# Weight sums of a seven-product scheme moved from VectorE into accumulating DMA transfers

## The chip, the cores and the metric

The kernel runs on one core of a Trainium2 chip. The metric is the device time of one execution in microseconds. TensorE does the matmuls, VectorE (DVE), ScalarE (ACT) and GpSimd (POOL) the elementwise work. Transfers are issued by SyncE (its queue is SP) and in a few places by GpSimd (its queue is POOL); all of them are carried out by the same 16 DMA engines of the core.

## The reference, cut to what matters

One inference step of a decoder layer on 576 tokens (512 of a prompt, 64 of a sample group). An RMS-normalised input is multiplied by the wide matrix `w_in`; its columns are split into attention, indexer, convolution and gate parts, and the two branches are merged and projected:

```python
c = split_columns(rms_norm(x, ln_g) @ w_in)        # 2048 x 10312
...
branch_attn = (attn * silu(c['z_attn'])) @ w_up_attn           # 1024 x 2048
u = c['glu_val'] * sigmoid(c['glu_gate'])                      # then a depthwise convolution over u
...
branch_conv = (conv_out * silu(c['z_conv'])) @ w_up_conv
merged = sigmoid(c['gate_attn']) * branch_attn + sigmoid(c['gate_conv']) * branch_conv
y = x + merged @ w_out
```

All values are float32. The kernel computes each float32 product as three matmuls: each operand is split into a high part (a cast to fp32r) and the remainder, and high x high, high x low and low x high are added.

## The kernel before

**Split.** `split` (lines 159 to 167) takes a weight tile `raw` of 128 partitions x 8 x 128: ACT casts it to `whi` (line 164) and DVE subtracts to make `wlo` (line 166). Both have three buffers, shared by everything that multiplies weights.

**Ordinary blocks.** `block` (line 248 has its matmul) multiplies such units with the normalised input for 576 tokens as two matmuls (256 and 320 columns) per weight and part. It is used up to about 660 us and from 1122 us on between the other products.

**Seven-product pairs.** `strassen` computes two neighbouring column blocks of 128 (`ca`, `cb`) for all tokens at once. The contraction is cut in two halves (`half` 0 and 1, `n` = 8 units of 128 rows each, 4 for `w_up_attn`) and the tokens in two halves of 288. The four weight quarters are b11 (half 0, ca), b12 (half 0, cb), b21 (half 1, ca) and b22 (half 1, cb). Seven products, each with one sum of weight quarters and one sum of input quarters (made once beforehand, lines 941 to 958 and 1083 to 1099), take the place of eight; a product is 24 matmuls of 288 columns (12 for `w_up_attn`; line 191). Its results are combined on DVE (line 201) and two copies on ACT (lines 205 and 210). The order is A11, S1, S2, S4, A12, S3, A22.

Four 512 KB loads from SP (line 178) bring the quarters, two into the two buffers of `wraw`, two into the two of `wx`. Four DVE instructions make the weight sums: t1 = b12 - b11 (line 207), t2 = b22 - t1 (212), b22 - b12 (217) and b21 - t2 (224).

There are 20 pairs over `w_in` (one for `z_conv`, three in the last three convolution tiles, eight for `gate_attn`, eight for `gate_conv`), which run back to back from 660 to 1122 us, and 8 pairs over `w_up_attn`, which alternate with ordinary blocks between 1155 and 1320 us. Beside the 20 pairs DVE also computes the depthwise convolution (`dw`, line 716) and the layer norm after it.

**Other transfers from GpSimd.** The attention gathers cache rows with indirect transfers on POOL (line 408): 128 rows of 1 KB each (`kic`, 128 KB) or 128 rows of 4 KB (`vc` and `kc`, 512 KB). Between 660 and 1600 us GpSimd has nothing to do.

**Order of the work.** The program gives each instruction a priority (`pri`): 0 for loading, summing and splitting weights, 1 for evictions, 3 and 5 for the attention and the convolution, 6 for the matmuls. The framework simulates the engines when it builds the program and fixes each engine's order by these priorities; on the chip each engine and each queue works in that order.

Of the kernel before, what the change touches and what calls it, by code (L numbers as in the profile page):

```python
# [9 lines left out]
F32 = mybir.dt.float32  # L10
# [4 lines left out]
OP = mybir.AluOpType  # L15
# [70 lines left out]
def build(tc, I, O):  # L86
    nc = tc.nc
    v, s, g, pe = nc.vector, nc.scalar, nc.gpsimd, nc.tensor
    dma = nc.sync.dma_start
# [3 lines left out]
    @contextmanager  # L93
    def pri(level):
        old = tc.cur_priority
        start = level * 1000000 + count.get(level, 0)
        tc.cur_priority = start
        yield
        count[level] = count.get(level, 0) + tc.cur_priority - start
        tc.cur_priority = old  # L100

    def ap(h, off, dims):
        return bass.AP(tensor=h.tensor, offset=h.offset + off, ap=[list(d) for d in dims])

    per = ctx.enter_context(tc.tile_pool(name="per", bufs=1))
# [63 lines left out]
    def strassen(pool, w, width, ca, cb, A, ev, kts=16, lvl=6, EV=1, rp=None):  # L169


        n = kts // 2
        with pri(0):
            raws = []
            for c0, half, tag in ((ca, 0, "wraw"), (cb, 0, "wraw"), (ca, 1, "wx"), (cb, 1, "wx")):
                t = (per.tile([128, 8, 128], F32, name="wraw", tag="wraw", bufs=2) if tag == "wraw" else
                     (rp or pool).tile([128, 8, 128], F32, name="wx", tag="wx", bufs=2))[:, :n]
                dma(t, ap(w, half * n * 128 * width + c0, [[width, 128], [128 * width, n], [1, 128]]))
                raws.append(t)
            b11, b12, b21, b22 = raws  # L180
            t1 = pool.tile([128, n, 128], F32, name="t1", tag="wt", bufs=2)
            t2 = pool.tile([128, n, 128], F32, name="t2", tag="wt", bufs=2)

        def product(raw, x):
            p = ps.tile([128, 512], F32, name="mms", tag="mm", bufs=4)[:, :T2]
            with pri(0):
                hi, lo = split(raw)
            with pri(lvl):
                for k in range(n):
                    for j, (a, part) in enumerate(((hi, 0), (hi, 1), (lo, 0))):  # L190
                        pe.matmul(p, a[:, k], A[x](part, k), start=(k == 0 and j == 0), stop=(k == n - 1 and j == 2))  # L191
            return p

        def kept():
            return pool.tile([128, T2], F32, name="sk", tag="sk", bufs=5)

        k1, k5, u2, v2 = (kept() for _ in range(4))

        def add(out, a, b):
            with pri(EV):  # L200
                v.tensor_add(out, a, b)  # L201

        p = product(b11, "A11")
        with pri(EV):
            s.copy(k1, p)
        with pri(0):
            v.tensor_sub(t1, b12, b11)
        p = product(t1, "S1")
        with pri(EV):
            s.copy(k5, p)  # L210
        with pri(0):
            v.tensor_sub(t2, b22, t1)
        p = product(t2, "S2")
        add(u2, p, k1)
        p = product(b22, "S4")
        with pri(0):
            v.tensor_sub(b22, b22, b12)
        add(v2, u2, k5)
        add(v2, p, v2)
        with pri(EV):  # L220
            ev(0, 1, v2)
        p = product(b21, "A12")
        with pri(0):
            v.tensor_sub(b21, b21, t2)
        add(k1, p, k1)
        with pri(EV):
            ev(0, 0, k1)
        p = product(b22, "S3")
        add(u2, p, u2)
        add(k5, u2, k5)  # L230
        with pri(EV):
            ev(1, 1, k5)
        p = product(b21, "A22")
        add(u2, p, u2)
        with pri(EV):
            ev(1, 0, u2)
# [47 lines left out]
    with tc.tile_pool(name="p0", bufs=1) as p0, pri(-1):  # L284
# [11 lines left out]
        def load(i):  # L296
            for cs in (slice(0, D // 2), slice(D // 2, D)):
                dma(xt[i][:TILES[i][1], cs], xrows(i)[:, cs])
# [27 lines left out]
        for h, tiles in enumerate(((0, 1), (2, 3, 4))):  # L326
            for i in tiles:
                n = TILES[i][1]
                for k, (eng, c0, c1) in enumerate(SQ[i]):
                    x, out = xt[i][:n, c0:c1], ss[:n, i, k:k + 1]  # L330
# [7 lines left out]
            with pri(-2):  # L338
# [7 lines left out]
                for c0, c1, eng in SCALE:  # L346
                    for k, i in enumerate(tiles):
                        x = xt[i][:TILES[i][1], c0 * 128:c1 * 128]
                        n = TILES[i][1]
                        (g if eng == "P" else v).tensor_scalar(x, x, rr[:n, k:k + 1], rt[:n, k:k + 1],  # L350
                                                               op0=OP.mult, op1=OP.mult)
            for kt in range(16):
                tag = PT_TAGS[h][kt % len(PT_TAGS[h])]
                pt = ps.tile([128, 512], F32, name="pt", tag=tag, bufs={"mm": 4, "w": 3, "o": 1}[tag])
                for i in tiles:
                    t0, n = TILES[i]
# [9 lines left out]
        for q in range(4):  # L366
            rows = slice(q * 32, (q + 1) * 32)
# [12 lines left out]
    CH, TK, EV = 3, 5, 1  # L380
# [31 lines left out]
    p = block(I["w_in"], D_IN, C_KI, xin, 72, units=units)  # L412
# [12 lines left out]
    with pri(CH):  # L425
# [15 lines left out]
        wt = p1.tile([128, 4, 8], F32, name="wt", tag="qh", bufs=2)  # L441
# [17 lines left out]
    for c in range(4):  # L459
        p = ps.tile([128, 512], F32, name="mm1", tag="mm", bufs=4)  # L460
# [8 lines left out]
        with pri(EV):  # L469
            s.copy(qi[:, c], p[:, NW:NQ])  # L470
            for e in range(2):
                rows = slice(e * 64, (e + 1) * 64)
# [107 lines left out]
    for kv in range(2):  # L580
        p = win(C_K + 128 * kv)
# [353 lines left out]
    with pri(CH):  # L935
        for q in range(4):
            c = slice(2 * q, 2 * q + 2)
            fs = [p4.tile([128, 2, T2], F32, name="f", tag="f", bufs=4) for _ in range(4)]
            whole(fs[0], quarter(1, 0), c)
            whole(fs[1], quarter(1, 1), c)  # L940
            v.tensor_add(fs[1], fs[0], fs[1])
            whole(fs[2], quarter(0, 0), c)
            parts(s1, fs[1], c)
            v.tensor_sub(fs[2], fs[1], fs[2])
            whole(fs[3], quarter(0, 1), c)
            parts(s2, fs[2], c)
            v.tensor_sub(fs[3], fs[3], fs[2])
            parts(s4, fs[3], c)
        for q in range(4):
            c = slice(2 * q, 2 * q + 2)  # L950
            f0, f1 = (st("f").rearrange("p (k t) -> p k t", k=2) for _ in range(2))
            whole(f0, quarter(0, 0), c)
            whole(f1, quarter(1, 0), c)
            v.tensor_sub(f0, f0, f1)
            parts(quarter(1, 0), f0, c)
# [116 lines left out]
    with pri(CH):  # L1072
        for k in range(4):
            t1, t2 = st("al"), st("al")
            dma(t1, a_d[k])
            dma(t2, a_d[k + 4])
            x11, x21, x12, x22 = t1[:, TS2[0]], t1[:, TS2[1]], t2[:, TS2[0]], t2[:, TS2[1]]

            def put(name, src):
                o = UA[name]  # L1080
                s.copy(o[:, 0, k], src)
                v.tensor_sub(o[:, 1, k], src, o.bitcast(F32)[:, 0, k])

            def new():
                return pU.tile([128, T2], F32, name="sk", tag="sk", bufs=5)

            f1, f2, f3, f4 = (new() for _ in range(4))
            put("A11", x11)
            v.tensor_sub(f3, x11, x21)
            put("S3", f3)  # L1090
            v.tensor_add(f1, x21, x22)
            put("S1", f1)
            v.tensor_sub(f2, f1, x11)
            put("S2", f2)
            put("A12", x12)
            put("A22", x22)
            v.tensor_sub(f4, x12, f2)
            put("S4", f4)
    XU = {a: (lambda part, k, o=o: o[:, part, k]) for a, o in UA.items()}
    cT = per.tile([128, 2, 8, T], R, name="cT", tag="x1")  # L1100
# [190 lines left out]
```

## Time and profile before

| | |
|---|---|
| runs (3) | 1604.26 to 1605.88 us, median 1605.86 us |
| profiled execution, its time | 1602.39 us |
| its span, first to last instruction | 1600.5 us |
| mean granted TensorE clock | 0.992 of full |
| data moved by DMA | 228.96 MB |

The profile lists for each engine how long it was busy and what it waited for. "PE" is TensorE's matmul side, "PEld" its weight loads, which overlap the matmuls. A busy TensorE says little by itself, since matmuls are pipelined; how many matmuls a stretch holds says more.

### The profile page before, as it was taken

How to read it: one execution, taken by the hardware profiler on the slowest of the kernel's cores; microseconds unless marked ns; L12 is line 12 of the kernel's file. 1: busy time of each engine (PE TensorE's matmuls, PEld its weight loads, DVE VectorE, ACT ScalarE, POOL GpSimd, SP SyncE). 2: the span in 40 equal slices, each digit the busy share in tenths (PEclk: the TensorE clock that was granted, in tenths of full speed). 3: DMA queues.
4: the chain of work that ended last, by engine and by line, in shares of the span. 5: the costliest groups of instructions: out<-in, count | busy, mean ns of one | idle time of the engine just before them, and what ended most of it. 6: DMA issues, size and time to landing. Idle time of an engine off the chain costs nothing.

```text
span 1600.5 us, 28485 instructions
## 1 busy us (share of the span) xinstructions
PE 1562.8 (98%) x11474; PEld 1517.9 (95%) x11474; DVE 1186.8 (74%) x2051; ACT 694.8 (43%) x1169; POOL 60.8 (4%) x81
## 2 busy tenths in 40 slices
PE   7999999999999999999999999999999999999997
PEld 5889999899989999999999999999999999999996
DVE  5436996365849599999999999899877675445554
ACT  5444324535455432344343345657533232334443
POOL 4200100101111000000000000000000000000000
PEclk8999999999999999999999999999999999999998
DMA  6632534434444334334343453644655666855773
GB/s 197 184 110 67 173 112 123 135 103 129 135 140 118 87 85 113 111 111 124 91 123 94 137 164 110 182 121 133 198 176 173 195 199 189 257 162 145 209 199 107
DMA packets 323827, 228.96 MB, mean 143 GB/s; under 512 B 15317, under 2 KB 293973, under 8 KB 322976
## 3 DMA queue, kind: packets, MB, share of 16 engines
q1 hardware_dynamic: 321008, 217.71, 46.6%
q0 software_dynamic: 2688, 9.44, 1.8%
q8 instruction: 90, 1.47, 0.4%
q14 instruction: 41, 0.34, 0.1%
HBM read 193.53 MB, written 36.96 MB: 144 GB/s over the span
## 4 chain that ended last, share of the span: by engine, by line
PE 88%; DVE 6%; issue 2%; DMA 2%; ACT 1%; POOL 0%; ACTq 0%; DVEq 0%; POOLq 0%
PE mm L248 51%; PE mms L191 26%; PE mm L467 2%; DVE wlo L166 2%; PE po L796 1%; DVE dw L716 1%; PE po L865 1%; PE pw L778 1%; DMA wx<-in_w_pw 1%; DVE sk L201 1%; PE pw L792 1%; PE pw L1209 1%; PE pw L527 1%; PE pw L828 0%; PE pt L357 0%
## 5 line engine op out<-in xcount | busy, mean ns | idle before, releaser
L248 PE MATMUL mm<-x,whi 128*128 128x256 f32 (+2 forms) x2368 | 430.6, 298 | 0.0
L248 PEld LDWEIGHTS mm<-x,whi 128*128 128x128 f32 (+1 forms) x2368 | 358.6, 187 | 5.8 <-issue 3.9
L164 ACT CAST whi<-wraw 128x1024 fp32r<-128x1024 f32 (+2 forms) x154 | 157.3, 1022 | 282.5 <-PE mm L248 203.5
L248 PE MATMUL mm<-x,wlo 128*128 128x256 f32 (+3 forms) x1184 | 260.3, 297 | 0.0
L191 PE MATMUL mms<-x,whi 128*128 128x288 f32 x1280 | 255.4, 296 | 4.3 <-DVE x L933 1.7
L166 DVE TENSOR_TENSOR wlo<-wraw,whi 128x1024 fp32r<-128x1024 f32 (+2 forms) x154 | 183.4, 1191 | 86.6 <-ACT whi L164 86.0
L164 ACT CAST whi<-wx 128x1024 fp32r<-128x1024 f32 (+1 forms) x156 | 150.0, 962 | 196.9 <-PE mm L248 53.4
L166 DVE TENSOR_TENSOR wlo<-wx,whi 128x1024 fp32r<-128x1024 f32 (+1 forms) x156 | 173.3, 1111 | 64.9 <-ACT whi L164 62.6
L191 PEld LDWEIGHTS mms<-x,whi 128*128 128x128 f32 x1280 | 204.5, 189 | 6.0 <-DVE x L933 2.1
L248 PE MATMUL mm<-m,whi 128*128 128x320 f32 (+1 forms) x1024 | 208.0, 298 | 0.0
L248 PEld LDWEIGHTS mm<-x,wlo 128*128 128x128 f32 (+1 forms) x1184 | 198.5, 187 | 0.7 <-issue 0.2
L191 PE MATMUL mms<-x,wlo 128*128 128x288 f32 x640 | 188.0, 297 | 3.5 <-DVE wlo L166 3.5
L191 PE MATMUL mms<-s,whi 128*128 128x288 f32 x960 | 191.4, 295 | 0.0
L716 DVE SCALAR_TENSOR_TENSOR dw<-u,cp,dw 128x512 f32<-128x512 f32 x240 | 178.2, 749 | 1.5
L248 PEld LDWEIGHTS mm<-m,whi 128*128 128x128 f32 x1024 | 164.3, 189 | 0.1
L191 PEld LDWEIGHTS mms<-s,whi 128*128 128x128 f32 x960 | 153.3, 188 | 0.1
L248 PE MATMUL mm<-m,wlo 128*128 128x320 f32 (+1 forms) x512 | 151.2, 296 | 0.0
L191 PE MATMUL mms<-s,wlo 128*128 128x288 f32 x480 | 140.9, 296 | 0.9 <-DVE wlo L166 0.9
L191 PEld LDWEIGHTS mms<-x,wlo 128*128 128x128 f32 x640 | 120.0, 189 | 5.3 <-DVE wlo L166 5.2
L164 ACT CAST whi<-t 128x1024 fp32r<-128x1024 f32 (+1 forms) x56 | 51.9, 927 | 110.5 <-PE mm L248 59.5
L248 PEld LDWEIGHTS mm<-m,wlo 128*128 128x128 f32 x512 | 96.4, 188 | 0.0
L191 PEld LDWEIGHTS mms<-s,wlo 128*128 128x128 f32 x480 | 89.9, 188 | 1.6 <-DVE wlo L166 1.5
(317 smaller groups left out, 2283.5 us busy)
## 6 DMA issues: line engine op xcount, KB each, us to landing
wraw<-in_w_in SPq DMA_DIRECT2D x120, 512.0 KB
wx<-in_w_in SPq DMA_DIRECT2D x40, 512.0 KB
wraw<-in_w_out SPq DMA_DIRECT2D x32, 512.0 KB
wx<-in_w_out SPq DMA_DIRECT2D x32, 512.0 KB
ga<-ga_d SPq DMA_DIRECT2D x32, 288.0 KB
ga_d<-gt SPq DMA_DIRECT2D x16, 288.0 KB
gc_d<-gt SPq DMA_DIRECT2D x16, 288.0 KB
gc<-gc_d SPq DMA_DIRECT2D x16, 288.0 KB
```

What stands on the lines that cost most here:

```text
L164: s.copy(hi, raw[:, :, :n])
L166: v.tensor_sub(lo, raw[:, :, :n], hi.bitcast(F32))
L191: pe.matmul(p, a[:, k], A[x](part, k), start=(k == 0 and j == 0), stop=(k == n - 1 and j == 2))
L201: v.tensor_add(out, a, b)
L248: pe.matmul(p[h][:n, :HN[h]], a[:, k, :n], x(part, kt, h), start=(kt == 0 and j == 0), stop=(kt == kts - 1 and j == 2))
L467: pe.matmul(p[:, :NQ], a[:, k], xk(part, kt)[:, 128:], start=(kt == 0 and j == 0), stop=(kt == 15 and j == 2))
L527: pe.matmul(d0[:, :W], qdup(part, h)[:, (i - 1) * 128:i * 128], kst[:, :W], start=(part == 0), stop=(part == 1))
L716: v.scalar_tensor_tensor(o1, a1, k1, o1, op0=OP.mult, op1=OP.add)
L778: pe.matmul(S[:, :max(W, 256)], a, x[:, kv, :max(W, 256)], start=(j == 0), stop=(j == 2))
L792: pe.transpose(pt[:, b * 128:(b + 1) * 128], Lt[:, b * 128:(b + 1) * 128], ident)
L796: pe.matmul(out[:, i * 128:(i + 1) * 128], vt[:, b, kv * 128:(kv + 1) * 128], PT[:, b * 128:(b + 1) * 128], start=(b == 0), stop=(b == i))
L865: pe.matmul(out[q:q + 32, :128], PT[:, r, q:q + 32], vc[:, b2, r * 256 + kv * 128:r * 256 + kv * 128 + 128], start=(r == 0), stop=False, t ...
```

## The change

The quarters b11, b21 and b22 are loaded from SP as before, and a tile `t` is loaded with b12. All weight sums are then made in place by DMA transfers that add what they read from HBM to what stands in the tile (`accum_op=OP.add`), issued by GpSimd: t += b11 gives the weight of S1; after S1's split t += b22 gives that of S2; after S2's split t += b21 gives that of A22; and after S4's split b22 += b12 gives that of S3. So that there are sums only, some signs change: two of the sums of input quarters and two of the combinations of products turn from an addition to a subtraction or the other way round. The order of the products becomes A11, S1, S4, S2, A12, S3, A22. The tag `wx` now has one tile per pair in its two buffers, `wt` too; `wraw` two as before.

```diff
+        def load(tile, half, c0):
+            dma(tile, rows(half, c0))
+            return tile
+
+        def more_of(tile, half, c0):
+            with pri(0):
+                g.dma_start(out=tile, in_=rows(half, c0), accum_op=OP.add)
...
+            b11 = load(shape(per, "wraw"), 0, ca)
+            t = load(shape(pool, "wt", n), 0, cb)
+            more_of(t, 0, ca)
+            b22 = load(shape(rp or pool, "wx"), 1, cb)
+            b21 = load(shape(per, "wraw"), 1, ca)
...
         p = product(b11, "A11")
         with pri(EV):
             s.copy(k1, p)
-        with pri(0):
-            v.tensor_sub(t1, b12, b11)
-        p = product(t1, "S1")
+        p = product(t, "S1")
+        more_of(t, 1, cb)
         with pri(EV):
             s.copy(k5, p)
-        with pri(0):
-            v.tensor_sub(t2, b22, t1)
-        p = product(t2, "S2")
+        p = product(b22, "S4")
+        more_of(b22, 0, cb)
+        add(v2, p, k5)
+        p = product(t, "S2")
+        more_of(t, 1, ca)
         add(u2, p, k1)
-        p = product(b22, "S4")
-        with pri(0):
-            v.tensor_sub(b22, b22, b12)
-        add(v2, u2, k5)
-        add(v2, p, v2)
+        sub(v2, v2, u2)
         with pri(EV):
             ev(0, 1, v2)
         p = product(b21, "A12")
-        with pri(0):
-            v.tensor_sub(b21, b21, t2)
         add(k1, p, k1)
...
         p = product(b22, "S3")
         add(u2, p, u2)
-        add(k5, u2, k5)
+        sub(k5, k5, u2)
...
-        p = product(b21, "A22")
+        p = product(t, "A22")
         add(u2, p, u2)
...
-            v.tensor_add(fs[1], fs[0], fs[1])
+            v.tensor_sub(fs[1], fs[0], fs[1])
...
-            v.tensor_sub(fs[3], fs[3], fs[2])
+            v.tensor_add(fs[3], fs[3], fs[2])
...
-            v.tensor_add(f1, x21, x22)
+            v.tensor_sub(f1, x21, x22)
...
-            v.tensor_sub(f4, x12, f2)
+            v.tensor_add(f4, x12, f2)
```

## Rows read from the trace of the kernel before

**Rows 1.** The page: busy time by engine; the chain by engine.
```profile
PE 1562.8 (98%) x11474; PEld 1517.9 (95%) x11474; DVE 1186.8 (74%) x2051; ACT 694.8 (43%) x1169; POOL 60.8 (4%) x81
...
PE 88%; DVE 6%; issue 2%; DMA 2%; ACT 1%; POOL 0%; ACTq 0%; DVEq 0%; POOLq 0%
```

**Rows 2.** Windows of the two stages with pairs (660:1122, 1155:1320).
```profile
core 0: us, PE busy (x) PEld busy (x) DVE busy (x) ACT busy (x) POOL busy (x), PEclk, DMA share, GB/s
660.00:1122.00 462.00, 453.29 (x3378) 448.89 (x3378) 439.63 (x611) 221.82 (x328) 0.00 (x0) 1.00 0.43 124
...
1155.00:1320.00 165.00, 160.39 (x1180) 158.38 (x1179) 122.81 (x232) 58.11 (x100) 0.00 (x0) 0.99 0.60 181
```

**Rows 3.** Windows of 40 us inside the first stage, same columns.
```profile
840.00:880.00 40.00, 37.44 (x280) 36.73 (x278) 38.78 (x53) 15.25 (x22) 0.00 (x0) 1.00 0.35 94
920.00:960.00 40.00, 40.00 (x304) 40.00 (x303) 37.36 (x51) 17.77 (x25) 0.00 (x0) 1.00 0.56 164
```

**Rows 4.** Waits of PE, 660:1122: us in total, times, longest us.
```profile
PE mms L191 <- DVE wlo L166: 4.4, 7, 1.2
PE mms L191 <- DVE x L933: 1.7, 2, 1.4
PE mms L191 <- ACT sk L210: 1.6, 2, 0.8
PE mms L191 <- ACT whi L164: 1.1, 2, 0.6
```

**Rows 5.** DVE's groups by line, 660:1122: count, busy us, mean ns, idle before.
```profile
L166 DVE TENSOR_TENSOR wlo<-wx,whi 128x1024 fp32r<-128x1024 f32 x80 | 97.5, 1219 | 4.4 <-ACT whi L164 4.3
L716 DVE SCALAR_TENSOR_TENSOR dw<-u,cp,dw 128x512 f32<-128x512 f32 x101 | 74.9, 746 | 0.0
...
L217 DVE TENSOR_TENSOR wx<-wx,wraw 128x1024 f32<-128x1024 f32 x20 | 24.4, 1219 | 0.1
```

**Rows 6.** ACT's waits, 660:1122, for its casts of weights.
```profile
ACT whi L164 <- PE mms L191: 74.2, 46, 2.5
...
ACT whi L164 <- DVE wx L217: 22.6, 8, 4.4
ACT whi L164 <- DVE t L212: 15.3, 11, 4.1
ACT whi L164 <- DVE wx L224: 9.6, 5, 3.1
```

**Rows 7.** ACT's groups by line, 660:1122.
```profile
L164 ACT CAST whi<-wx 128x1024 fp32r<-128x1024 f32 x80 | 83.9, 1050 | 94.0 <-PE mms L191 26.9 <-issue 25.1 <-DVE wx L217 22.6
```

**Rows 8.** The gathers' line, L408, on POOL: duration ns min/median/max; then their landing.
```profile
L408 POOL DMA_INDIRECT kic<-in_cache_kidx,idx x8: 944/946/1515, 51.5 to 62.5; - x8
L408 POOL DMA_INDIRECT vc<-in_cache_v,idx x8: 937/947/1942, 160.1 to 469.9; - x8
...
DMA to landing us min/median/max: 2.7/4.2/6.4
```

**Rows 9.** DMA, 300:520: queues (packets, MB, share); issues with us to landing.
```profile
q1 hardware_dynamic: 32405, 22.16, 35.1%
q0 software_dynamic: 1584, 5.77, 8.1%
...
vc<-in_cache_v,idx POOLq DMA_INDIRECT x6, 4.6
kc<-in_cache_k,idx POOLq DMA_INDIRECT x5, 4.7
```

**Rows 10.** DMA, 660:1122: the queue of SP, and the loads of weights.
```profile
q1 hardware_dynamic: 90487, 56.52, 42.6%
...
wx<-in_w_in SPq DMA_DIRECT2D x38, 512.0 KB
```

**Rows 11.** Waits of SP's queue, 660:1122.
```profile
SPq L178 <- DVE wx L217: 70.0, 12, 13.8
SPq L178 <- DVE wlo L166: 67.6, 26, 8.6
```

**Rows 12.** POOL's groups by line: gathers' idle time between two in a row.
```profile
L408 POOL DMA_INDIRECT kic<-in_cache_kidx,idx x8 | 8.3, 1043 | 15.6 <-DVE sc L514 11.9 <-ACT kip L499 2.2 <-issue 1.2
```

More of the change, by code (lines that the diff above doesn't have):

```diff
@@ L172, in strassen, with rows, shape @@
         n = kts // 2
-        with pri(0):
[L174 to L182, printed above, removed]
+        def rows(half, c0):
+            return ap(w, half * n * 128 * width + c0, [[width, 128], [128 * width, n], [1, 128]])
+        def load(tile, half, c0):
[4 more added lines that the diff above has]
+                g.dma_start(out=tile, in_=rows(half, c0), accum_op=OP.add)
+        def shape(p, tag, k=8):
+            return p.tile([128, k, 128], F32, name=tag, tag=tag, bufs=2)[:, :n]
+        with pri(0):
+            b11 = load(shape(per, "wraw"), 0, ca)
[3 more added lines that the diff above has]
+            b21 = load(shape(per, "wraw"), 1, ca)
         def product(raw, x):
@@ L201, in add, with sub @@
                 v.tensor_add(out, a, b)
+        def sub(out, a, b):
+            with pri(EV):
+                v.tensor_sub(out, a, b)
         p = product(b11, "A11")
```

## The prediction, on record before the changed kernel ran

> **What bounds the kernel now.** Read first the page's busy times and its chain by engine [rows 1]: TensorE is busy for 98% of the span and holds 88% of the chain, DVE 6%. So a change that leaves all 11474 matmuls as they are can win only where TensorE waits. Next read the windows of the two stages that hold pairs [rows 2]: from 660 to 1122 us DVE is busy for 439.63 of 462 us (95%), TensorE for 453.29. These are two engines close to their limit in one stage; DMA is at 0.43 and POOL is empty. What TensorE loses there is told best by counts: a stretch without a loss holds 304 matmuls in 40 us, one at 840 us holds 280 [rows 3]. The pace without loss is 40 / 304 = 0.1316 us, so 3378 matmuls need 444.5 us and the stage loses at most 17.5 us (a few of them are shorter transposes). The waits give the other bound: 4.4 + 1.7 + 1.6 + 1.1 = 8.8 us, most of it for a `wlo` that DVE made late [rows 4]. One step back, ACT's casts wait 22.6 + 15.3 + 9.6 = 47.5 us for the weight sums that the change takes off DVE, and 74.2 us for matmuls to free a buffer of `whi` [rows 6]. The second number says that splits mostly run as far ahead as three buffers allow; where they don't, DVE is the reason.
>
> **DVE's part.** Four sums per pair go, at 1.219 us each [rows 5]: 20 x 4 x 1.219 = 97.5 us of the 439.6. DVE would be at 342 of 462 us, 74%. The seven combinations per pair stay seven, and the sums of input quarters only change their signs: nothing. The 74.9 us of convolution in these rows is work of lower priority that already fills gaps, and can be pushed around. With that, the waits of rows 4 for `wlo`, for the copies and for the casts should go: 8.8 us at least, 17.5 at most; I take 12, two thirds of the upper bound, since the sums stand right ahead of the casts that wait.
>
> **SP's part.** Four loads per pair stay on SP. They now wait less for buffers: the 70.0 us for line 217 [rows 11], which kept b12 in its buffer, go, and `t` and b22 have two buffers for one tile per pair, so that they and the first sum can be fetched a whole pair ahead. No gain of its own, since no row shows TensorE waiting for these loads; it is cover for what follows.
>
> **POOL's part: three prices that the trace doesn't show.** Four adding transfers of 512 KB per pair, 80 in the first stage, and 32 of 256 KB in the second. A transfer here has 1024 runs of 512 B, the gathers have 128 rows.
>
> First, the time on POOL to issue one. The gathers took 0.946 us with 1 KB rows and 0.947 with 4 KB rows [rows 8]: bytes don't matter, rows may. If all of it were per row, one takes 8 x 0.946 = 7.6 us; if all of it were fixed, 0.95. I take 1.9, twice the nearest row, as each run has to be read from two places. Four of them with the 0.3 us between two gathers (1.2 us over 4 gaps) [rows 12] make 8.8 us of a pair's 462 / 20 = 23.1: it fits. The Trainium skill ("DMA: Bandwidth & Descriptors", Anatomy of one DMA) says that many descriptors can be emitted before the incremental cost shows up; by that the sum would stand at the lower end, and no run here shows it.
>
> Second, the share of the DMA engines. SP's packets cost 0.426 x 16 x 462 us / 56.52 MB = 55.7 us per MB of one engine [rows 10], the gathers' 0.081 x 16 x 220 / 5.77 = 49.4 [rows 9]. 512 KB (0.524 MB) over 16 engines is then 1.6 us for a plain copy at POOL's price and 1.8 at SP's; an adding one has to read its destination as well, so up to twice, 3.65. I take 2.6, half way: 80 x 2.6 = 208 us of 462, 0.45 on top of 0.43, which makes 0.88. In the second stage 32 x 1.3 = 42 us of 165, 0.25 on top of 0.60.
>
> Third, the time from issue to landing, for the chain is now through memory: S1's split, a transfer, S2's split, a transfer, A22's split. A product is 24 x 0.1316 = 3.16 us. S1's split can start when the product three before it (S3 of the last pair) has freed its buffer, and takes 1.05 us on ACT [rows 7] and 1.22 on DVE. TensorE then still has A22, A11, S1 and S4 to do, 12.6 us, and S2's cast takes 1.05. So a transfer that lands within 12.6 - 2.27 - 1.05 = 9.3 us costs nothing. The 512 KB gathers landed in 4.6 and 4.7 us [rows 9]. Adding 0.95 for the dearer issue and 2.6 - 1.6 = 1.0 for the second read gives 6.6: hidden. With the upper prices it is 4.6 + 6.6 + 2.0 = 13.2: not. The transfers for A22 and S3 have more room: from S4 to S3 three products lie, and from S2's split to A22 two.
>
> In the second stage products last half as long (1.58 us), but an ordinary unit of 48 matmuls stands ahead of each pair, 48 x 165 / 1180 = 6.7 us [rows 2]; with a split of half the size (1.14 us, its cast 0.53), S1's room is 6.7 + 3 x 1.58 - 1.14 - 0.53 = 9.8 us for 256 KB. After it, at some 6 us per landing, A22's room is nearly used up, so I charge a quarter of a microsecond for each of 8 pairs, 2 us (nothing to 8 us). Its own loss of 4.6 us I leave.
>
> **The sum.** -12 + 2 = -10 us on the profiled execution, 1602.4 to 1592.4. The runs' median is 3.5 us above that execution, so 1605.9 - 10 = 1596 on the median's scale. If all goes well, -17.5 - 4.6 = -22 (1584); with the lower bound and 8 us given back, -1 us.
>
> **Rivals.** *POOL the bound (slower).* If issuing goes with runs, POOL becomes the bound: the point is (23.1 / 4) - 0.3 = 5.5 us for one. At 6.5 us, a pair takes 4 x 6.8 = 27.2 us, 20 x 4.1 = +82 us: 1688; at 7.6, over 1770. For it: nothing in rows 8 says how much of the 0.95 us is fixed, since all gathers have 128 rows. Against it: they are no dearer with four times the bytes, and POOL is otherwise empty in this stage [rows 2].
>
> *DMA engines full (slower).* At 3.65 us each, 292 us on top of 0.43 x 462 = 199 us make 491 us of work in a stage that else needs 450: +29 us, 1635. It decides from (450 - 199) / 80 = 3.1 us per transfer on. For it: the second stage has 0.60 already [rows 2], and small packets cost more per byte (55.7 against 49.4). Against it: what POOL's queue moved was the cheaper of the two. The Trainium skill ("Collectives: The Full Stack", Why ReduceScatter is half of AllGather) says that an add inside a DMA engine is slow not for the arithmetic but for its two source reads, which halve the rate; by that rule each transfer costs twice a copy's 1.6 to 1.8 us, and the time comes out between no gain and this rival. No run of the kernel before shows an adding transfer.
>
> *Landing too late (slower).* If only the landing exceeds 9.3 us, by 1.5 us say, S2 is late once per pair: 20 x 1.5 - 12 = +18 us, 1624. The cast of S2 would then also hold up the casts behind it in ACT's queue, and `wlo` those in DVE's, though both have a quarter of their time free.
>
> *No difference.* The waits of rows 4 are replaced by equal ones for landings, or the fixed order of ACT and DVE, laid out when the program is built, is off by what it gained: within 3 us of 1606.
>
> **Chances.** The forecast 0.44, no difference 0.15, POOL 0.15, DMA full 0.13, late landing 0.13. Three slower cases together are nearly as likely as the forecast, as three unknown prices must all be low for it; but each alone is less likely. Faster by over 0.2% (3.2 us, about what a measurement of this kernel can tell): 0.44; same 0.15; slower 0.41. The forecast's own range is 1584 to 1602. The whole range reaches from 1584 to 1650: it takes in the late landing and most of the full DMA engines, and leaves out most of the POOL case, where the time runs off to 1690 and beyond.
>
> **What the next profile would show.** Right: lines 207, 212, 217 and 224 gone from DVE, its busy time in the stage near 342 us, DMA_DIRECT2D on POOL near 2 us with landing under 9 us, a DMA share below 0.95, waits of TensorE for `wlo` near nothing, and 300 or more matmuls in nearly every 40 us. Wrong: POOL's issues of 5 us and more back to back; or casts of `t` and `wx` on ACT waiting for landings with TensorE behind them; or loads by SP that land late, with the DMA share at its top. In the first stage, a pair's period above 23.1 us shows at once that one of the three prices was too low. The sums leave DVE in any case; what can be wrong is where their time goes.

## The result, and the profile after

The changed kernel takes 1734.25 us (median of 4 runs, 1732.54 to 1739.32), the kernel before 1605.87 us beside it (4 runs): a ratio of 1.0811, interval 1.0792 to 1.083. The forecast was 1596 us, faster, and its range ended at 1650: wrong in sign and outside the range. The profiled execution took 1732.54 us with a span of 1730.8.

The page of the changed kernel: busy time by engine, the chain by engine, and the group of casts that waited most (the first two answer [rows 1]).

```profile
PE 1610.3 (93%) x11474; PEld 1552.8 (90%) x11474; DVE 1086.8 (63%) x1939; ACT 692.5 (40%) x1169; POOL 226.2 (13%) x193
...
PE 51%; DMA 27%; issue 7%; DVE 7%; ACT 4%; POOL 2%; SPq 0%; ACTq 0%; POOLq 0%; DVEq 0%
...
L164 ACT CAST whi<-wt 128x1024 fp32r<-128x1024 f32 (+1 forms) x84 | 77.6, 924 | 317.5 <-DMA wt<-in_w_in 235.2
```

DVE is busy for 100 us less (1186.8 to 1086.8), and the lines of the four sums are gone from it. But TensorE holds 51% of the chain instead of 88%, and transfers hold 27% instead of 2%. The casts of `wt`, the tile that carries the running sum, waited 235.2 us for transfers.

Windows of the two stages with pairs, of 40 us in the first, and of two products (answering [rows 2, 3]); columns as there. The first window ends before its stage does.

```profile
660.00:1170.00 510.00, 447.94 (x3082) 437.66 (x3081) 335.68 (x501) 198.57 (x296) 112.07 (x74) 0.93 0.97 178
1250.00:1440.00 190.00, 166.57 (x1177) 159.67 (x1176) 108.56 (x220) 59.59 (x113) 38.34 (x30) 0.97 0.84 194
...
880.00:920.00 40.00, 33.86 (x240) 32.80 (x240) 28.31 (x40) 13.13 (x19) 10.98 (x8) 0.95 1.00 161
```
```profile
909.20:912.30 3.10, 3.10 (x25) 2.98 (x23) 0.62 (x1) 0.00 (x0) 0.29 (x1) 1.00 1.30 243
916.60:923.10 6.50, 6.06 (x24) 5.72 (x25) 6.50 (x8) 2.26 (x3) 1.54 (x1) 0.52 0.59 76
```

TensorE does 240 matmuls in 40 us, where a stretch without loss holds 304. The first stage now runs from 661.2 to 1219.6 us (first to last matmul of a pair over `w_in`), 558.4 us instead of 462.3: 27.9 us for a pair instead of 23.1. The second takes 180.4 us (1259.9 to 1440.3) instead of 155.1. That is 96 + 25 of the 130 us; 7 more lie between the two stages. The last two rows are two products of one pair, S4 and S2, with 24 matmuls of the same shape: 3.1 us for the first at the upper clock level (granted 1.00), 6.5 us for the second, after TensorE had stood for 4.3 us, at the lower one (0.52).

The waits, 660 to 1170 us (answering [rows 4, 6]): engine, line, releaser, us in total, times, longest us.

```profile
ACT whi L164 <- DMA wt<-in_w_in: 206.0, 32, 9.4
POOL wt L184 <- DVE wlo L166: 156.9, 23, 13.1
...
POOL wt L184 <- DMA wt<-in_w_in: 78.3, 7, 14.5
...
PE mms L203 <- ACT whi L164: 50.6, 18, 6.7
...
ACT whi L164 <- PE mms L203: 19.2, 12, 5.6
```

Before, ACT's casts waited 74.2 us for TensorE to free a buffer: splits ran ahead. Now it is 19.2, and TensorE waits for the casts. POOL's adds wait for splits (156.9) and, 78.3 us, for the load of the tile that they add to, each at the head of POOL's queue. Where does TensorE lose? For each of the 3360 matmuls of the first stage's pairs I took the time since the start of the matmul ahead of it, less the pace of 0.1316 us, and summed by product what exceeds it by more than 0.05 us (us):

```
           A11   S1   S4   S2  A12   S3  A22   sum
before     1.6  0.0  0.1  3.0  0.2  5.7  3.8  14.4
changed    0.2  0.0  8.3 94.8  0.9  0.6  4.7 109.4
```

The 95 us by which the sums differ are the 96 by which the stage grew, and nearly all stand at S2, the first product whose weights come by a transfer that starts only after another split. Of its 94.8 us, 66.9 stand ahead of its first three matmuls; the rest is S2 running slowly after the stop, as in the windows. In all TensorE ran for 117 us at the lower clock level (granted 0.50), against 28 before.

One pair of the changed kernel in time: POOL's and then ACT's timeline (start us, us, what; idle time before it and its releaser).

```profile
878.54 3.11 POOL L184 DMA_DIRECT2D wt<-in_w_in  x2 [13.11 <-DVE wlo L166]
881.02 2.21 POOL L184 DMA_DIRECT2D wx<-in_w_in  x1
890.56 1.54 POOL L184 DMA_DIRECT2D wt<-in_w_in  x1 [7.33 <-DVE wlo L166]
```
```profile
878.35 1.06 ACT L164 CAST whi<-wx 128x1024 fp32r<-128x1024 f32 x1 [2.15 <-PE mms L203]
...
887.76 1.05 ACT L164 CAST whi<-wt 128x1024 fp32r<-128x1024 f32 x1 [8.01 <-DMA wt<-in_w_in]
...
889.00 1.05 ACT L164 CAST whi<-wraw 128x1024 fp32r<-128x1024 f32 x1
...
897.22 1.06 ACT L164 CAST whi<-wt 128x1024 fp32r<-128x1024 f32 x1 [4.55 <-DMA wt<-in_w_in]
```

S1's split ends at 877.95. POOL then issues three adds within 2.5 us: the next pair's first sum (which also waits for SP's load of that pair's tile), S2's, and S3's (into `wx`). S2's lands for its cast at 887.76, 9.8 us after the split. The fourth, for A22, is issued alone at 890.56, and its cast starts at 897.22: 6.7 us. ACT stands for 8.01 us at the head of its queue, with A12's cast behind.

### The profile page after: what moved, and what is told of

It reads as the page before. It is cut to its first block, busy times and chain, and to the rows that moved or that the text cites. A ratio compares the mean times of both kernels' runs of the same rounds, so it can differ in the third digit from the quotient of the medians.

```text
span 1730.8 us, 28690 instructions
## 1 busy us (share of the span) xinstructions
PE 1610.3 (93%) x11474; PEld 1552.8 (90%) x11474; DVE 1086.8 (63%) x1939; ACT 692.5 (40%) x1169; POOL 226.2 (13%) x193
## 4 chain that ended last, share of the span: by engine, by line
PE 51%; DMA 27%; issue 7%; DVE 7%; ACT 4%; POOL 2%; SPq 0%; ACTq 0%; POOLq 0%; DVEq 0%
PE mm L259 40%; DMA wt<-in_w_in 19%; DMA wt<-in_w_up_attn 5%; DVE wlo L166 3%; PE mms L203 3%; ACT whi L164 3%; PE mm L478 1%; DVE dw L727 1%; POOL wt L184 1%; PE po L807 1%; PE po L876 1%; PE pw L789 1%; DMA wraw<-in_w_out 1%; DMA wraw<-in_w_in 1%; DMA wx<-in_w_up_attn 1%
## 5 line engine op out<-in xcount | busy, mean ns | idle before, releaser
L164 ACT CAST whi<-wraw 128x1024 fp32r<-128x1024 f32 (+2 forms) x182 | 182.9, 1006 | 261.1 <-PE mm L259 205.8
L166 DVE TENSOR_TENSOR wlo<-wraw,whi 128x1024 fp32r<-128x1024 f32 (+2 forms) x182 | 213.2, 1171 | 90.8 <-ACT whi L164 89.1
L203 PE MATMUL mms<-s,whi 128*128 128x288 f32 x960 | 220.2, 325 | 52.9 <-ACT whi L164 52.9
L203 PEld LDWEIGHTS mms<-s,whi 128*128 128x128 f32 x960 | 175.8, 214 | 57.0 <-ACT whi L164 56.9
L166 DVE TENSOR_TENSOR wlo<-wt,whi 128x1024 fp32r<-128x1024 f32 (+1 forms) x84 | 89.9, 1071 | 193.4 <-ACT whi L164 193.2
L164 ACT CAST whi<-wt 128x1024 fp32r<-128x1024 f32 (+1 forms) x84 | 77.6, 924 | 317.5 <-DMA wt<-in_w_in 235.2
L166 DVE TENSOR_TENSOR wlo<-wx,whi 128x1024 fp32r<-128x1024 f32 (+1 forms) x100 | 113.6, 1136 | 85.7 <-ACT whi L164 83.6
L203 PE MATMUL mms<-s,wlo 128*128 128x288 f32 x480 | 156.6, 327 | 10.1 <-DVE wlo L166 10.1
L164 ACT CAST whi<-wx 128x1024 fp32r<-128x1024 f32 (+1 forms) x100 | 98.0, 980 | 160.3 <-PE mm L259 90.0
L184 POOL DMA_DIRECT2D wt<-in_w_in x60 | 93.3, 1670 | 512.9 <-DVE wlo L166 182.9
```

The source lines that it names most:

```text
L164: s.copy(hi, raw[:, :, :n])
L166: v.tensor_sub(lo, raw[:, :, :n], hi.bitcast(F32))
L184: g.dma_start(out=tile, in_=rows(half, c0), accum_op=OP.add)
```

## The experiments

Three theories at first, with the letters that the expectations use. A: the added transfers land later than forecast, and the casts that need them wait. B: the 16 DMA engines are full, whoever waits. C: it is something else in the change (POOL, the product order, the buffers).

**Copies in place of adds.**

```diff
-                g.dma_start(out=tile, in_=rows(half, c0), accum_op=OP.add)
+                g.dma_start(out=tile, in_=rows(half, c0))
```

> Leaves out the adding: the same transfers on the same queue with the same waits, as plain copies (the weight sums are then not sums). Theory A (each pair waits for two landings in series, S1's split to S2's and S2's to A22's, and a landing takes 9 to 10 us because an adding packet of 512 B takes 66 ns): a copy's packets take 27 to 30 ns, landings come to 5 to 6 us, two of them and some 7 us of splits make 17 to 19 us per pair, under TensorE's 22.1; 1590 to 1610 us. Theory B (the 16 DMA engines are full, whoever waits): 1.7 us in place of 4.3 per transfer leaves the engines at 0.75, also 1590 to 1615. Theory C (issuing on POOL, the new order of products or sums in place cost the time, not the adding): stays above 1700.

1613.25 us (one run; before 1603.55). The same 112 transfers, queue, waits and order, and 121 us are gone. So theory C is out as the main cause; A and B both forecast this. The queue of GpSimd from 660 to 1120 us, here, and from 660 to 1170 us in the changed kernel, with the landings:

```profile
q0 software_dynamic: 11092, 40.38, 30.0%
...
wt<-in_w_in POOLq DMA_DIRECT2D x57, 512.0 KB, 4.9
```
```profile
q0 software_dynamic: 73961, 37.28, 59.7%
...
wt<-in_w_in POOLq DMA_DIRECT2D x55, 512.0 KB, 9.9
...
wx<-in_w_in POOLq DMA_DIRECT2D x19, 512.0 KB, 9.4
```

A copy: 0.300 x 16 x 460 us / 40.38 MB = 54.7 us of one engine per MB, 1.79 us of all 16 for 512 KB. An add: 0.597 x 16 x 510 / 37.28 = 130.7 per MB, 4.28 us. So an add costs 2.4 copies, and more than my upper bound of 3.65. The packets say how: copies travel in packets of 3.6 KB on average (40.38 MB / 11092), adds in 504 B, one for each run of 512 B, each of about 66 ns. (These are the packets' recorded times, and they can overlap, as the run of adds that nobody reads shows below.) The window of the copies from 660 to 1120 us:

```profile
660.00:1120.00 460.00, 450.49 (x3345) 446.09 (x3345) 352.84 (x523) 217.84 (x322) 68.78 (x77) 1.00 0.73 209
```

**All four sums on VectorE, in the new order.** This keeps the order, signs and tags of the change; b12 stays in one of the two buffers of `wt`, the first sum goes into the other, and the other three sums are made in place.

```diff
-            more_of(t, 0, ca)
+            b12 = t
+            t = shape(pool, "wt", n)
+            v.tensor_add(t, b12, b11)
...
-        more_of(t, 1, cb)
+        with pri(0):
+            v.tensor_add(t, t, b22)
```

(and the same for S3's and A22's sums.)

> The new signs, the new order of products and the sums in place, but all four sums on VectorE again, no adding transfer. Theories A and B: within 10 us of the kernel before, 1597 to 1615. Theory C (order or sums in place): above 1650.

1598.24 us (9 runs), ratio 0.9965 [0.9955, 0.9975]: 0.35% faster than the kernel before. The window 660 to 1120:

```profile
660.00:1120.00 460.00, 452.21 (x3375) 448.58 (x3374) 439.53 (x611) 222.79 (x327) 0.00 (x0) 1.00 0.42 123
```

DVE is as full as before (439.53 of 460 us, 96%), and TensorE loses 12.6 us by the count above, against 14.4. Most of the gain stands in the second stage, 148.0 us against 155.1. What a lighter DVE would give, this run can't tell.

**The same with the old product order.**

```diff
+        p = product(t, "S2")
+        add(u2, p, k1)
         p = product(b22, "S4")
-        add(v2, p, k5)
-        p = product(t, "S2")
-        add(u2, p, k1)
-        sub(v2, v2, u2)
+        sub(v2, k5, u2)
+        add(v2, p, v2)
```

> All sums on VectorE, in place and with the new signs and buffers, but in the old order A11, S1, S2, S4, A12, S3, A22. The version in the new order took 1598 us, the kernel before 1604. If the order gave the 5.6 us, this one takes 1602 to 1608; if the buffers and the sums in place did, 1596 to 1600.

1601.67 us (10 runs), 0.9985 [0.9976, 0.9995]. The order is worth 0.2% (0.9985 against 0.9965, intervals just apart), the buffers and in-place sums 0.15%. Both were costed at nothing.

**How many adds, and which.** Each of these puts some of the four sums on VectorE, in place, and leaves the others as adds: two adds (first sum, S3's); one (S3's); three without S2's; three without the first; and only S2's and A22's, with b11 for b12 in S3's sum, since b12 is then overwritten. The edit is this one, for the sums named:

```diff
-        more_of(t, 1, cb)
+        with pri(0):
+            v.tensor_add(t, t, b22)
```

> Two of the four sums stay adding transfers, those that nobody needs soon (t += b11 a pair ahead, b22 += b12 between S4 and S3); S2's and A22's are made in place by VectorE. Theory A: no landing in series is left, VectorE is relieved of 49 us in the first stage: 1590 to 1603, faster than before. Theory B: two adds of 4.3 us and 8 us of loads and 3 of stores are 19.6 of 22.5 us, just below full: 1600 to 1640.

1611.86 us (5 runs), 1.0049 [1.0035, 1.0063].

> Only b22 += b12 stays an adding transfer, three products ahead of its use; the other three sums are made in place by VectorE, in the new order. No other add stands before it on POOL's queue. Both theories: landing near 6 us within a room of 13, 0.55 to 0.65 of the engines: 1592 to 1602, at or a little below the version with all sums on VectorE (1598). If S3's cast still waits for it, a rule of its own is at work.

1616.13 us (6 runs), 1.007 [1.0056, 1.0085]. The expectation was missed, and one add is no cheaper than two: the first sum, made a pair ahead, adds nothing. In both runs ACT waits for S3's sum in the first stage (53.9 us for `wx` with two adds, 64.7 with one), but TensorE hardly follows: with two adds this stage takes 459.8 us, with one 465.5, and with all sums on VectorE 460.1. Most of what the adds cost here stands in the second stage, 165.1 and 161.1 us against 148.0, where TensorE loses 12.5 and 10.0 us at S3.

> Only S2's sum goes back to VectorE, in place; three adds per pair stay and one landing is left in the chain from S1's split to A22's. Theory A: a pair's chain is one landing of 8 to 10 us and some 10 us, below TensorE's 22.1; what is left are late landings for S3 and A22: 1605 to 1630. Theory B: three adds of 4.3 and 11 us of other packets are 24 us per pair: 1630 to 1660.

1635.18 us (one run; before 1604.0).

> Three adds per pair, as in the version with three adds measured at 1635 us, but another one goes back to VectorE: the first sum (t += b11, a pair ahead), not S2's. The two adds in series, S1 to S2 to A22, stay. Theory A (the wait in series): 1685 to 1725, near the full change, though a fourth of its adds is gone. Theory B (packet time of the engines): the same number of adds, the same time, 1625 to 1645.

1682.31 us (one run; before 1605.12).

> Two adds per pair, the two in series (S2's and A22's sums); the first sum and S3's are on VectorE (S3's adds b11 for b12, so the output is not the reference's). Its counterpart with the two other adds took 1612 us. Theory A: 1650 to 1700, slower than the version with three adds of which one is in series. Theory B: 1605 to 1620, as its counterpart.

1692.58 us (one run; before 1605.12). The waits of this last one, 660 to 1170 us:

```profile
ACT whi L164 <- DMA wt<-in_w_in: 190.6, 40, 10.2
...
PEld mms L203 <- ACT whi L164: 33.6, 25, 3.4
```

ACT waits 40 times, twice per pair, for landings in `wt`, and TensorE's weight loads 25 times for the casts behind them. Two adds cost 8 us or 87 us, three cost 31 or 77. What decides is not the number but whether both S2's and A22's sums, which stand between two splits of the same tile, are among them: there every landing waits for a split and a split for the landing.

**The adds off the chain.** S2's split reads b11 and A22's b21, so that no cast waits for the sums of `t` after the first; all adds stay.

```diff
-        p = product(t, "S2")
+        p = product(b11, "S2")
...
-        p = product(t, "A22")
+        p = product(b21, "A22")
```

> All four adding transfers per pair stay, in the same places, but S2 and A22 are split from the tiles b11 and b21, so nobody waits for the second and third add (the products are then not the reference's). Theory A (the wait in series): gone, 1595 to 1620 us. Theory B (engines full): the traffic is the same, so 1700 to 1735 stay. In between, by how much each holds.

1681.71 us (one run; before 1603.55): better by 53 us, but no cure. The adds into `t` now wait for each other or for SP's load of their tile (101.8 and 163.0 us of the first row, by who issued the transfer), and S3's add into `wx` behind them in POOL's queue, so that ACT waits for it (waits, 660 to 1170):

```profile
POOL wt L184 <- DMA wt<-in_w_in: 264.8, 35, 13.5
ACT whi L164 <- DMA wx<-in_w_in: 122.2, 19, 11.5
```

**Adds that nobody reads.** No split reads an added tile.

```diff
-        p = product(t, "S1")
+        p = product(b11, "S1")
...
-        p = product(t, "S2")
-        more_of(t, 1, ca)
+        p = product(b11, "S2")
+        more_of(b22, 1, ca)
...
-        p = product(b22, "S3")
+        p = product(b21, "S3")
...
-        p = product(t, "A22")
+        p = product(b21, "A22")
```

> All four adding transfers per pair go to the same queue with the same bytes, but no product reads a tile that an add writes (S1 and S2 are split from b11, S3 and A22 from b21; the third add goes to b22's tile, so that no three adds follow one another on one tile; the products are not the reference's). Theory A (waits for landings): no such wait is left, 1593 to 1610 us. Theory B (engines full): four adds of 4.3 us and some 11 us of loads and stores per pair are still 28 us of packet time against TensorE's 22.1: 1650 to 1735.

1704.24 us (one run; before 1604.0). The adds now wait for no split and come in denser; the plain loads of `wraw` are late instead (ACT's casts waited 114.5 us for them from 660 to 900 us), and once most adds are through, TensorE runs near its pace. The windows of the two parts:

```profile
660.00:900.00 240.00, 186.15 (x1270) 181.47 (x1270) 146.72 (x211) 69.45 (x100) 79.96 (x52) 0.87 1.26 208
900.00:1220.00 320.00, 307.63 (x2278) 305.68 (x2277) 227.71 (x351) 163.64 (x251) 43.94 (x29) 0.98 0.79 170
```

1270 matmuls in 240 us are 212 in 40; 2278 in 320 are 285. This fits theory B's range, but it doesn't show the engines to be the cause, for a chain is left: SP's queue works in order, and before it loads `wt` or `wx` again it waits for the adds into that buffer, with the loads of `wraw` behind. SP's waits from 660 to 930 us:

```profile
SPq L178 <- DMA wt<-in_w_in: 113.2, 18, 17.1
SPq L178 <- DMA wx<-in_w_in: 91.2, 8, 28.0
```

A DMA share of 1.26 also says that the share is no gauge with a stop at 1: an engine's packets overlap in the records.

**A control, and the adds into a tile of their own.** The control has all sums on VectorE and one buffer for `wt`; the other run adds the four transfers into a tile `off` that nobody reads.

```diff
+            more_of(off, 0, ca)
...
+        more_of(off, 1, cb)
...
+        more_of(off, 0, cb)
...
+        more_of(off, 1, ca)
```

> The control for the next one: all sums on VectorE in place, one buffer for t in place of two, S3's sum adds b11 for b12. Both theories: 1596 to 1612.

1621.35 us (one run; before 1605.12).

> The control with all four adds per pair issued as well, into a tile that no instruction reads and no load waits for, one in flight at a time. Nothing but the DMA engines connects them with the pairs. Theory A: within 15 us of the control. Theory B: 28 us of packets per pair against 22.1 of matmuls, 60 us or more above the control.

1746.92 us, but as a whole this run is inconclusive. 81.8 us of it is one wait after the first stage: DVE's zeroing of the second stage's `off` waits 81.7 us for the lagging adds, and ACT and TensorE wait behind it:

```profile
PE mm L271 <- ACT whi L165: 83.5, 3, 81.8
```

The first stage alone took 512 us, 37 more than the control's 475 and far less than the changed kernel's 558. It loses them at S1 (37.3 us against 9.1 in the control), whose tile is loaded late beside the adds. By the end of the stage 67 of its 80 adds had been issued. No load and no cast waits for them, so these 37 us are what the runs show of the DMA engines' part alone, for a kernel with one buffer of `wt`.

**Runs of 4 KB.** The adds read one run of 4 KB per partition, 128 in place of 1024 (other weights are summed).

```diff
-                g.dma_start(out=tile, in_=rows(half, c0), accum_op=OP.add)
+                g.dma_start(out=tile.rearrange("p k c -> p (k c)"),
+                            in_=ap(w, half * n * 128 * width + min(c0, width - 128 * n), [[width, 128], [1, 128 * n]]),
+                            accum_op=OP.add)
```

> The adding transfers read one run of 4 KB per partition (other columns of the same matrix, so the sums are not the reference's) where they read eight of 512 B; bytes, places and waits stay. If the 65 ns of an adding packet are mostly a price per packet, a 4 KB packet takes 200 to 250 ns, a landing 5 to 6 us, and the time comes to 1605 to 1630. If it is a price per byte, a packet takes 500 ns and the time stays at 1700 to 1740.

1673.07 us (one run; before 1604.0), between the two ranges expected. The queue from 660 to 1170 us:

```profile
q0 software_dynamic: 11196, 40.75, 45.1%
...
wt<-in_w_in POOLq DMA_DIRECT2D x57, 512.0 KB, 6.2
```

0.451 x 16 x 510 / 40.75 = 90.3 us per MB, 2.96 us for 512 KB. So with packets as large as a copy's an add costs 1.65 copies; the rest of the 2.4 is that short runs are not put together when they are added. Nearly half of the loss, 61 us, goes with it.

**More room for S2.** If S2's sum is late against its room, give it room: with the order S1, S4, A11, S2, one more product lies between S1's split and S2.

```diff
-        p = product(b11, "A11")
-        with pri(EV):
-            s.copy(k1, p)
         p = product(t, "S1")
...
         add(v2, p, k5)
+        p = product(b11, "A11")
+        with pri(EV):
+            s.copy(k1, p)
         p = product(t, "S2")
```

> All four adds per pair, correct sums, with A11 moved from the first place to the third: S1, S4, A11, S2, A12, S3, A22, so that S1 and S2 have two products between them in place of one, 3.2 us more room for the add in series. Theory A (room for S2's landing): S2's loss falls from 95 us to 10 to 40, the time to 1630 to 1670. Theory B (packet time of the engines): 1710 to 1735.

1736.36 us (one run; before 1604.2): nothing gained, just above theory B's range. The same with the first sum on VectorE:

```diff
-            more_of(t, 0, ca)
+            v.tensor_add(t, t, b11)
```

> The same order with the first sum on VectorE, three adds per pair. If the add issued right ahead of S2's makes it late, S2's loss goes to under 10 us and the time is 1615 to 1640, clearly below the one with four; if not, both are within 10 us of each other.

1657.27 us (one run), 25 less than with three adds in the other order: S2's loss went as expected (2.6 us), but the time is above the range, for 21.9 us now stand at A12. Why did room help with three adds and not with four? POOL's timeline with four:

```profile
825.15 3.10 POOL L184 DMA_DIRECT2D wt<-in_w_in  x2 [12.02 <-DMA wt<-in_w_in]
826.92 2.90 POOL L184 DMA_DIRECT2D wx<-in_w_in  x1
```

The queue's order has the next pair's first sum ahead of S2's, and that one waits for the load of its tile. S1's split had ended at 823.33; S2's add left at 826.03, 2.7 us late, and landed with two others 11.3 us after that. The room had grown from 8.1 to 10.7 us, but the way from S1's split to S2's cast from 10.2 to 14.1.

**The first sum behind A22's add in POOL's queue.** All four adds; only that order is fixed.

```diff
-            more_of(t, 0, ca)
+            with tc.issue_after(last[0].ins) if last else nullcontext():
+                more_of(t, 0, ca)
...
-        more_of(t, 1, ca)
+        last[:] = [more_of(t, 1, ca)]
```

In the order with more room:

> Product order S1, S4, A11, S2, A12, S3, A22 as in the run with more room (1736 us), all four adds, but on POOL's queue the first sum of the next pair goes behind this pair's A22 add; there it went ahead of S2's add. In that run S2's add was issued 2.8 us after S1's split had ended (POOL stood at the first sum, which waits for the load of its tile), and landed 11.3 us later together with two others; S2's cast came 14.1 us after the split (median), the room was 10.7. Theory A (place in the queue: what counts is what is issued ahead of S2's add and beside it): S2's cast comes 8 to 9 us after the split, TensorE loses under 20 us at S2 instead of 84, and the time is 1640 to 1680 (three adds in this product order gave 1657). Theory B (the DMA engines are simply full: four adds of 4.2 us and four loads of 1.8 us are 24 us of all 16 engines for a pair that otherwise takes 22.3 to 23.1): the wait only moves to another product, and the time stays above 1710.

1679.39 us (4 runs), 1.0468 [1.045, 1.0485]: 57 us less, from a place in a queue. And in the changed kernel itself:

> The changed kernel, with nothing else changed than that the first sum of the next pair goes behind this pair's A22 add on POOL's queue. In the changed kernel S2's cast came 10.2 us after the end of S1's split (median), and TensorE could have used it after 8.1. Theory A: S2's cast comes 8 to 9 us after the split, the loss at S2 falls from 95 us to between 20 and 50, and the time is 1670 to 1700 (with the first sum on VectorE it was 1682). Theory B: within 15 us of the changed kernel's 1734. Both allow that S1 now waits, since its sum is issued later; the loss would then stand at S1.

1690.54 us (4 runs), 1.0549 [1.0525, 1.0574]: 44 us less. POOL's timeline of the former, and its DMA from 660 to 1170 us:

```profile
845.04 3.11 POOL L186 DMA_DIRECT2D wt<-in_w_in  x2 [4.39 <-DVE wlo L166]
861.82 1.54 POOL L186 DMA_DIRECT2D wt<-in_w_in  x1 [13.67 <-DMA wt<-in_w_in]
864.18 1.54 POOL L186 DMA_DIRECT2D wx<-in_w_in  x1 [0.83 <-DVE wlo L166]
```
```profile
DMA packets 171503, 97.90 MB, mean 192 GB/s; under 512 B 3501, under 2 KB 166599, under 8 KB 171463
```

S2's add (861.82) leaves alone, S3's 2.4 us behind it, and the next pair's first sum only with A22's (the two at 845.04). The engines moved 192 GB/s here against 178 in the changed kernel, with all four adds: they had not been at their end before. The medians over 19 pairs, in us (way: from the end of S1's split to the start of S2's cast; room: from there to the end of the product ahead of S2, less 1.05 for the cast):

```
                                     way   room   S2's loss   all losses   run
changed                             10.2    8.1        94.8        109.4   1734
first sum behind A22's               7.6    6.9        51.2         73.0   1691
no first sum's add                   7.4    8.0        32.5         60.7   1682
more room                           14.1   10.7        83.6        111.0   1736
more room, first sum behind A22's    7.1    8.5         5.0         57.8   1679
more room, no first sum's add        7.2   10.6         2.6         39.8   1657
copies                               6.9    8.4        11.5         15.7   1613
```

Where the way is shorter than the room by 1.4 us or more, S2 loses 2.6 to 11.5 us; where it is longer, S2 loses 51 to 95 us; in between, 32.5. With more room and the queue in order the loss has left S2 and stands at S1 (26.6), whose sum is now issued last, and A22 (15.7).

## Why the prediction was wrong, by its own steps

- **The step that failed** is the third price: "Adding 0.95 for the dearer issue and 2.6 - 1.6 = 1.0 for the second read gives 6.6: hidden." Alone, an add does take that: 6.5 us with two adds per pair, 6.7 from A22's issue to its cast. But I costed a transfer by itself. S2's is issued beside the next pair's first sum and S3's, and three of 4.28 us are 12.8 us of all 16 engines. The landing became 9.9 us, the way to the cast 10.2; and the room was 8.1 in place of 9.3. The text had said that the first sum can "be fetched a whole pair ahead" and counted it as cover: that same fetch is what S2's add met. The two runs that move it show this: 44 and 57 us.
- **The engines' price** was mis-sized: 2.6 taken, 3.65 at most, 4.28 measured. I bounded it by "up to twice" SP's price, and SP's packets are short as well (56.52 MB / 90487 = 625 B on average [rows 10]). For plain copies the packet's size hardly mattered, 55.7 us per MB there against 54.7 in packets of 3.6 KB; for adds it did, 130.7 in runs of 512 B against 90.3 in runs of 4 KB. On the rule of the Trainium skill ("Collectives: The Full Stack", Why ReduceScatter is half of AllGather) that two reads halve the rate: with 4 KB runs an add cost 1.65 copies, near it; with these, 2.4. At 4.28 us my rival of full engines would have said 80 x 4.28 + 199 - 462 = +79 us, where the stage grew by 96. It names a true cost (67 adds beside the control's first stage cost it 37 us) but not the bound: with the same transfers the engines moved 189 and 192 GB/s once the queue was in order, against 178.
- **What a late sum costs** was taken as its delay, 20 x 1.5 us. The late landing was the right rival with the wrong price. S2 was late by 2.9 us in the median, 66.9 us in all, and after the stop TensorE ran at the lower clock level: 6.5 us for a product of 3.1. I had no term for that; 27.9 us of S2's loss are of this kind.
- **The gain of 12 us** from a lighter DVE shows in no run's sum. With copies DVE is at 352.84 us of 460, and TensorE loses 15.7; with two adds 12.3; with all sums on DVE 12.6, against 14.4 before. But 13.6 of the copies' 15.7 stand at S2 and S4, and the other five products lose 2.0 us where they lost 11.3 before. So part of the loss that I laid on DVE may have gone, with waits for landings in its place; no run with a lighter DVE is free of such waits, and this stays open. DVE's own share was reckoned a little high: from 660 to 1120 us it fell from 438.1 to 352.8, by 85 us for 97.5, since instructions in a row overlap in the records (the four lines' durations add up to 119.6 us in the whole kernel, the busy time fell by 100).
- **POOL's price** was right: 1.54 us an issue against 1.9 taken. That rival is out. The Trainium skill ("DMA: Bandwidth & Descriptors", Anatomy of one DMA) says that the incremental cost of descriptors shows up late; the trace agrees in part: 1.27 us with 512 runs, 1.54 with 1024.
- **The second stage**: +25 us for +2. Transfers into `wt` from `w_up_attn` hold 5% of the chain, but the losses are spread (S2 9.1, S3 8.9, A22 7.0, S4 6.4 us, by the count above), and plain copies cost it 7 us already (161.8 against 155.1). I had charged only A22.
- **The order costed at nothing** is worth 0.2%, in the good direction.

Of the 130 us, then: the adding itself, in place of copies, is about 120 (one run of the copies). Some 44 of it is the first sum's place in POOL's queue, and 61 go if the same bytes are added in long runs; no run combines the two, so how far they overlap is not shown. How the 75 us that are left with the queue in order (1679 against 1605) divide between loaded engines and the chain of splits and landings stays open. The run that was meant to separate the two was spoilt by the wait at the end of its stage, and its first stage gives only the 37 us named above.

## What to carry to other kernels

Moving a sum from an engine with 5% to spare into a transfer exchanges 1.2 us of engine time for 7 to 10 us of delay, which pays only where nothing stands between its inputs and its user. Before costing a transfer's landing, write down what else will be on its queue and on the DMA engines within that time, prefetches of the next iteration above all: what is early and harmless by itself can be in front of what is urgent. And if an engine is 95% busy, look whether others really wait for it: the fastest version here (1598 us) keeps all sums on VectorE and takes only the new product order and buffers.

## What the runs showed of the hardware that I had not expected

- An adding transfer is carried in one packet per run of 512 B, about 66 ns each; a plain copy of the same runs on the same queue went in packets of 3.6 KB on average. Per byte 2.4 times a copy.
- Issuing on POOL, 1024 runs: 0.88 us as a copy, 1.54 as an add. From the line of the adds (duration ns min/median/max):

```profile
L184 POOL DMA_DIRECT2D wt<-in_w_in x60: 1532/1542/2400, 645.6 to 1204.2; - x60
L184 POOL DMA_DIRECT2D wt<-in_w_up_attn x24: 1267/1275/1822, 1235.5 to 1431.0; - x24
```

- The DMA share of the trace can exceed 1 (1.26 over 240 us).
- With 15 of the 16 stops of TensorE at S2 in the first stage (1.0 to 6.9 us each) the granted clock fell to 0.50 during that product, and S2's waits of 66.9 us cost 94.8.
